# The down projection's seven products in two PSUM banks per visit, with sums kept in PSUM and partial results read between

## The chip, the cores and the metric

The kernel runs on one core of one Trainium2 chip. The metric is the device time of one execution in microseconds, as the median of several runs. The kernel before takes 2273.95 us (three runs, 2269.09 to 2274.33).

The engines named here are TensorE (PE, with its weight loads as PEld), VectorE (DVE), ScalarE (ACT), GpSimd (POOL) and the queue that issues most loads (SP). ScalarE's and GpSimd's own instruction queues issue transfers too.

## The reference

One block of a hybrid network, float32, 512 tokens, model width 2048, feed-forward width 5632. The first part (input projection, a state-space mixer, a three-branch attention, output projection) is not touched. What matters here is the end:

```python
    h = h + mixed @ w_out[l]
    v = rmsnorm(h, ffn_norm_w[l])
    h = h + (jax.nn.silu(v @ w_gate[l]) * (v @ w_up[l])) @ w_down[l]
return rmsnorm(h, final_norm_w)
```

The outputs must match this in float32, so every large product is done as three passes: both factors are split into a high part in the rounded format fp32r and a low part (the remainder), and high x high, high x low and low x high are added.

## The kernel before

**Seven products instead of eight.** In the gate, up and down projections, a 2x2 block product (two blocks of weight rows by two of weight columns, against two halves of 256 tokens) is done by seven products M1 to M7 of sums of blocks, in the manner of Strassen and Winograd. The weight blocks are 11, 12, 21, 22; the sums are S1 = 21 + 22, S3 (from 21 and 11), 11 + S1 (for M6) and 12 + 11 + S1 (for M3, where block 11 already holds the sum). M1 takes 11, M2 12, M5 S1, M7 S3, M4 22. The sums of activations are formed once and kept: for gate/up in the tiles V0, VV (in u) and T, for down in a scratch tensor g_d in device memory.

**Stages.** Up to about 800 us: input projection, mixer, attention and half of the output projection. 800 to 893 us: the other half of the output projection. About 893 to 1792 us: gate/up, 22 tiles u = 0 to 21, each with a gate side (0) and an up side (1), seven products a side, eight k-steps a product. A k-step of gate/up has two matmuls: the high weights against high and low activations together (512 columns) and the low weights against the high ones (256). From about 1792 us: down.

**Down.** 35 visits (table `VISITS`): visit (j, n) adds n k-blocks to output block j. A k-step has three matmuls of 256 columns (lines 1172 to 1174: high x high, high x low, low x high). The first 33 visits run their products in the order `SEQ_D` = M1, M2, M6, M3, M7, M4, M5; the last two visits use `SEQ_END` with a bank for each product, and are interleaved by `put_last`. `BANK_D` says which half (256 columns) of which of a visit's four PSUM banks a product fills. After M1, M6, M7 and M5, when a bank is full, `d_after` and `d_add` have VectorE add it to the accumulators `H[j]` in SBUF: four reads of 512 elements and two of 256 in a visit (the first visit of a block copies with ScalarE). PSUM has eight banks here: six turn round under the names ps_g, ps_s, ps_t (`bank`).

**Order of the work.** From the output projection's second half on, the order of instructions is as written: `run_step` is one product. It first lets `feed` issue loads of g_d, runs `before`, then `prep(i + 2)`: for the product three ahead, `form` does the weight sum if there is one (VectorE, line 134) and the high part (ScalarE, line 122); for the product two ahead, the low part (VectorE, line 125). Then come the product's matmuls, with one `sch.tick()` a k-step, and `after`, its reads of PSUM. `tick` also moves background generators on: `g_forms(u)` forms the seven activation sums of a finished gate/up tile, and its `yield n` waits n k-steps. It ends with a store to g_d from ScalarE's queue (line 1454), six k-steps after the last low part. `silu(u, ...)` is another such generator.

**Gate/up reads.** BANK puts M1, M6, M7, M4 in one bank X, M5 and M3 in R, M2 in W. The results are chained: the next product of the same bank adds on, and ScalarE or VectorE reads the sum so far in between (M1 at line 1379, M6 at 1384, M2 at 1389, M5 at 1395, M7 and M3 by VectorE, M4 at 1411). So the next product in that bank must wait for that read.

**Ring of activations.** The tiles V0, VV and T are reused in down as seven slots for g_d, loaded in two halves (four and three of the seven sums) by `feed`, from ScalarE's queue (line 1548). A slot is loaded once its last reader is done by some steps (table `done`).

**Sums of weights in down.** S1 is formed in place by GpSimd (line 134, POOL) from 21 and 22; S3 by GpSimd in the first six visits, later by an adding transfer from GpSimd's queue (line 1109).

Of the kernel before, what the change touches and what calls it, by code (L numbers as in the profile page):

```python
# [11 lines left out]
ALU = mybir.AluOpType  # L12
# [100 lines left out]
def body(ctx, tc, xT, w_in, w_out, w_gate, w_up, w_down, w1k, w1v, cols, rows, kst, out):  # L113
# [1042 lines left out]
    def run_step(s):  # L1156
# [13 lines left out]
        for k in range(0 if s.wide else n):  # L1170
            ah, al = s.rhs(k)
            pe.matmul(q, h[:, k, :], ah, start=(k == 0), stop=False)  # L1172
            pe.matmul(q, h[:, k, :], al, start=False, stop=False)  # L1173
            pe.matmul(q, l[:, k, :], ah, start=False, stop=(k == s.blk.n - 1))  # L1174
            sch.tick()
# [145 lines left out]
    def banks(which):  # L1321
        got = {}

        def get(p):
            def g():
                b, h = which[p]
                if b not in got:
                    got[b] = bank()
                return got[b], got[b][:, 256 * h:256 * h + 256]
            return g  # L1330
# [32 lines left out]
    def gu_after(u, side, got):  # L1363
        both = u in (0, NP - 1)

        def after(pr):
            def ev(p):
# [7 lines left out]
                c4 = c.rearrange("p (a t) -> p a t", a=4)  # L1375
                if pr == M1:
                    if u:
                        got["W"] = bank()
                    act.activation(got["W"] if u else u2, p, AF.Copy)
                elif pr == M6:  # L1380
                    if u == 0:
                        add(dve, u2, got["W"], u2)
                        add(dve, c4[:, 0], u2[:, lo_h], u2[:, hi_h])
                    act.activation(u2, p, AF.Copy)  # L1384
                elif pr == M2:
                    if u and both:
                        fold(c4[:, 0], p)
                    elif u:
                        act.activation(wv[:, 0, :], p, AF.Copy)
                elif pr == M5:  # L1390
                    if u == 0:
                        dve.tensor_tensor(m5, p, m5, ALU.subtract)
                        add(dve, u2, p, u2)
                    else:
                        act.activation(m5, p, AF.Copy)
                elif pr == M7:
                    add(dve, m5, p, m5)
                    if u == 0:
                        add(dve, c4[:, 1:4:2], wv[:, :, lo_h], wv[:, :, hi_h])
                elif pr == M3:  # L1400
                    if u == 0:
                        act.activation(m5, p, AF.Copy)
                    else:
                        add(dve, u2, p, u2)
                        if both:
                            add(dve, c4[:, 1:4:2], wv[:, :, lo_h], wv[:, :, hi_h])
# [26 lines left out]
    def g_forms(u):  # L1433
# [5 lines left out]
        yield 10  # L1439
        a_hi(sg[:, 0, 0, :], g[:, 0, lo_h])  # L1440
        a_hi(sg[:, 1:3, 0, :], g[:, 1, :].rearrange("p (a t) -> p a t", a=2), scale=-1.0)
# [464 lines left out]
```

## Time and profile before

| | us |
|---|---|
| median of 3 runs | 2273.95 |
| the profiled execution's own time | 2275.06 |
| its span, first to last instruction | 2273.3 |
| PE busy | 2177.7 (96%) |
| PEld busy | 1916.4 (84%) |
| DVE busy | 1822.6 (80%) |
| ACT busy | 1187.4 (52%) |
| POOL busy | 426.1 (19%) |

Mean granted TensorE clock: 0.984. The page gives busy time per engine, the costliest groups, and who released whom; "idle before" of a group is the time that its engine stood still just before, and "waits" list pairs of a waiting instruction and what it waited for, with the total, the number of times and the longest. Matmuls are pipelined, and a matmul's end is modelled: two that follow each other overlap, so the distance of starts says how fast TensorE goes.

### The profile page before, as it was taken

Reading aid. Unit: us, or ns where it says so; the run is one execution under the profiler, and the core shown is the slowest. Engines: PE = TensorE matmul, PEld = TensorE weight load, DVE = VectorE, ACT = ScalarE, POOL = GpSimd, SP = SyncE. Lnnn points to the kernel's source line nnn. Section 1 sums busy time; section 2 is a strip of 40 time slices with the busy share of each in tenths; the row PEclk is TensorE's granted clock in tenths of the full one; section 3 lists DMA queues with packets and bytes.
Section 4 is the critical chain, followed back from the end, with each engine's and each line's share of the span. In section 5 each row is a group of like instructions: output and inputs, shape, how many; then the busy total and the mean of one; then the engine's idle time right before and its main releaser. Section 6 shows DMA issues by size and latency. Waiting matters only on the chain. (4 is left out here: it accounts for less than half of the span.)

```text
span 2273.3 us, 35008 instructions
## 1 busy us (share of the span) xinstructions
PE 2177.7 (96%) x12904; PEld 1916.4 (84%) x12904; DVE 1822.6 (80%) x2858; ACT 1187.4 (52%) x1961; POOL 426.1 (19%) x433
## 2 busy tenths in 40 slices
PE   7999999999989989999999999999999899999996
PEld 5888888888877777888888888888888899999996
DVE  7699766688888667878888788887887798988897
ACT  4564446567666544655555555555555443333453
POOL 2011224223133224000000100001000121221222
PEclk8999999999989999999999999999999999999999
DMA  5222343222413265787878878788787969796974
GB/s 176 93 70 75 128 136 103 75 85 73 137 60 125 69 223 166 227 219 219 236 211 248 219 219 236 211 249 219 219 236 212 333 236 307 189 297 180 300 190 134
DMA packets 168555, 417.17 MB, mean 184 GB/s; under 512 B 16592, under 2 KB 23520, under 8 KB 168384
## 3 DMA queue, kind: packets, MB, share of 16 engines
q1 hardware_dynamic: 99776, 252.24, 33.7%
q0 software_dynamic: 25888, 76.72, 17.2%
q10 hardware_dynamic: 42720, 85.99, 10.5%
q8 instruction: 101, 1.65, 0.3%
q14 instruction: 70, 0.57, 0.1%
HBM read 353.80 MB, written 57.41 MB: 181 GB/s over the span
## 5 line engine op out<-in xcount | busy, mean ns | idle before, releaser
L122 ACT ACTIVATE R<-Z 128x1024 fp32r<-128x1024 f32 (+4 forms) x457 | 420.8, 934 | 442.7 <-DVE Z L134 315.0
L125 DVE TENSOR_TENSOR R<-Z,R 128x1024 fp32r<-128x1024 f32 (+4 forms) x363 | 393.6, 1092 | 41.1 <-ACT R L122 30.5
L232 PE MATMUL ps_g<-u,whi 128*128 128x512 f32 x720 | 286.1, 397 | 0.2 <-DVE h L131 0.2
L234 PE MATMUL ps_g<-u,wlo 128*128 128x512 f32 x720 | 284.4, 395 | 0.0
L233 PE MATMUL ps_g<-u,whi 128*128 128x512 f32 x720 | 283.9, 394 | 0.0
L1168 PE MATMUL ps_s<-u,R 128*128 128x512 f32 (+1 forms) x1152 | 253.4, 349 | 26.8 <-ACT A L1384 26.3
L1168 PEld LDWEIGHTS ps_s<-u,R 128*128 128x128 f32 x1152 | 186.6, 188 | 60.0 <-ACT A L1384 32.9
L125 DVE TENSOR_TENSOR wlo<-wraw,whi 128x512 fp32r<-128x512 f32 x196 | 151.3, 775 | 66.0 <-ACT whi L122 65.4
L122 ACT ACTIVATE whi<-wraw 128x512 fp32r<-128x512 f32 x196 | 122.6, 626 | 134.4 <-PE ps_g L233 89.7
L234 PEld LDWEIGHTS ps_g<-u,wlo 128*128 128x128 f32 x720 | 135.6, 188 | 27.1
L232 PEld LDWEIGHTS ps_g<-u,whi 128*128 128x128 f32 x720 | 135.9, 189 | 26.0 <-DVE h L131 0.5
L233 PEld LDWEIGHTS ps_g<-u,whi 128*128 128x128 f32 x720 | 135.8, 189 | 25.4
L1168 PE MATMUL ps_t<-u,R 128*128 128x512 f32 x592 | 132.5, 350 | 0.0
L134 DVE TENSOR_TENSOR A<-ps_g,A 128x512 f32<-128x512 f32 (+1 forms) x114 | 73.9, 655 | 73.1 <-PE ps_g L1168 39.1
L1168 PE MATMUL ps_g<-u,R 128*128 128x512 f32 (+1 forms) x600 | 131.5, 348 | 0.0
L1168 PE MATMUL ps_g<-T,R 128*128 128x512 f32 (+1 forms) x584 | 126.9, 348 | 0.0
L1168 PE MATMUL ps_s<-T,R 128*128 128x512 f32 (+1 forms) x552 | 123.9, 351 | 0.0
L1172 PE MATMUL ps_g<-u,R 128*128 128x256 f32 (+1 forms) x353 | 115.1, 326 | 9.0 <-ACT R L122 7.1
L122 ACT ACTIVATE R<-A 128x1024 fp32r<-128x1024 f32 (+3 forms) x79 | 74.7, 946 | 92.3 <-DVE A L134 65.2
L1168 PE MATMUL ps_s<-V,R 128*128 128x512 f32 (+1 forms) x568 | 122.7, 347 | 0.0
L125 DVE TENSOR_TENSOR E<-Z,R 128x1024 fp32r<-128x1024 f32 x94 | 114.6, 1219 | 9.4 <-ACT R L122 6.5
L1173 PE MATMUL ps_g<-u,R 128*128 128x256 f32 (+1 forms) x353 | 114.1, 323 | 0.0
(484 smaller groups left out, 5702.8 us busy)
## 6 DMA issues: line engine op xcount, KB each, us to landing
Z<-in_w_gate SPq DMA_DIRECT2D x95, 512.0 KB, 5.5
Z<-in_w_up SPq DMA_DIRECT2D x94, 512.0 KB, 5.1
wraw<-in_w_in SPq DMA_DIRECT2D x164, 256.0 KB, 2.6
g_d<-A ACTq DMA_DIRECT2D x22, 1792.0 KB, 13.9
Z<-in_w_gate POOLq DMA_DIRECT2D x39, 512.0 KB, 5.6
Z<-in_w_up POOLq DMA_DIRECT2D x38, 512.0 KB, 7.4
Z<-in_w_down SPq DMA_DIRECT2D x58, 320.0 KB, 5.4
Z<-in_w_down SPq DMA_DIRECT2D x40, 384.0 KB, 4.1
```

Source lines behind the costliest of these rows:

```text
L122: act.activation(dst, src, AF.Copy, scale=scale)
L125: eng.tensor_tensor(dst, src, f(hi), ALU.subtract)
L134: eng.tensor_tensor(o, a, b, ALU.add)
L232: pe.matmul(p, hi_t[i][:, j, :], ah, start=(k == 0), stop=False)
L233: pe.matmul(p, hi_t[i][:, j, :], al, start=False, stop=False)
L234: pe.matmul(p, lo_t[i][:, j, :], ah, start=False, stop=(k == u.nk - 1))
L1168: pe.matmul(o, w, x, start=start, stop=(k == n - 1 and o is q), skip_group_check=not fresh[0])
L1172: pe.matmul(q, h[:, k, :], ah, start=(k == 0), stop=False)
L1173: pe.matmul(q, h[:, k, :], al, start=False, stop=False)
```

## The change

Down runs its products in the gate/up order `SEQ` = M1, M5, M6, M2, M7, M3, M4, in two banks a visit. In the first bank M6 fills the lower half, M1 the upper half, and M2 adds on to M1. In the second M5 fills the lower half, M3 adds on to it, M7 fills the upper half, M4 adds on to it. VectorE reads M1, M5 and M7 alone (256 elements each) before the next product is added, and M6 with M1+M2, and M5+M3 with M7+M4 (512 each). For that the sums of activations get other signs (`g_forms`) and another order (`G_POS`). Only the first matmul in a bank clears it (`fresh`).

Four things come along. The store to g_d is issued 16 k-steps, not 6, after the last low part. `feed` loads the first halves of the first five ring slots one step after their last reader, where it was three (and for the first two slots counted from a later reader). The first gate/up tile u = 0 runs in the order of `SEQ`, and the pieces of T that it needs (`t_piece`) come at steps 0, 1, 4, 5, 7, 9 instead of 1 to 6. In the last two visits the products get three banks (`BANK_END`), another order (M1, M7, M6, M2, M4, then M5 of both, M3 of both), and the final norm's sums over the first 256 tokens are taken after M5 of the one and turned into a row after M5 of the other.

```diff
-SEQ_D = [M1, M2, M6, M3, M7, M4, M5]
-BANK_D = {M1: (0, 0), M6: (1, 0), M2: (1, 1), M3: (2, 0), M7: (2, 1), M4: (3, 0), M5: (3, 1)}
+BANK_D = {M6: (0, 0), M1: (0, 1), M2: (0, 1), M5: (1, 0), M3: (1, 0), M7: (1, 1), M4: (1, 1)}
-G_POS = [0, 1, 2, 4, 3, 5, 6]
+G_POS = [0, 1, 4, 3, 2, 5, 6]
...
-            pe.matmul(q, h[:, k, :], ah, start=(k == 0), stop=False)
...
+            go = dict(skip_group_check=fresh == [False])
+            pe.matmul(q, h[:, k, :], ah, start=(k == 0 and fresh != [False]), stop=False, **go)
...
     def g_forms(u):
...
-        yield 6
+        yield 16
         nc.scalar.dma_start(g_d[u].rearrange("v p n -> p v n"), f(sg).rearrange("p v s t -> p v (s t)"))
...
-                t_piece(*[(0, 1), (1, 1), (2, 0), (2, 1), (3, 0), (3, 1)][n - 1])
+                t_piece(*PIECES[n])
...
-    both_sides(0, "011 111 0S1 012 112 1S1 0S3 1S3 022 122", [(i, p) for p in (M1, M2, M3) for i in range(2)] +
-               [(i, p) for p in (M6, M5, M7, M4) for i in range(2)])
+    both_sides(0, "011 111 0S1 1S1 012 112 0S3 1S3 022 122", [(i, p) for p in SEQ for i in range(2)])
...
-                at = max(done.get((n - GRING, half), i), later.get(n, 0))
-                if n < 2 and half == 0:
-                    at = done.get((n + 1 - GRING, 0), i)
-                if n < 5 and half == 1:
-                    at = done.get((4 - GRING, 0), i) + n // 2
-                if at + 3 > i:
+                at = max(done.get((n - GRING, half), i), later.get(n, 0)) + 3
+                if n < 5:
+                    at = done.get((n - GRING, 0), i) + 1 if half == 0 else done.get((4 - GRING, 0), i) + 3 + n // 2
+                if at > i:
...
-    def d_add(j, pr, p, first, last):
+    def d_add(j, pr, p, first):
...
         if pr == M1:
             if first:
-                act.activation(H[:, 0, :], p[:, 0:256], AF.Copy)
-                add(dve, H[:, 1, :], p[:, 0:256], H[:, 1, :])
+                act.activation(H[:, 0, :], p[:, hi_h], AF.Copy)
             else:
-                add(dve, H[:, 0:2, :], b2, H[:, 0:2, :])
-        elif pr == M6:
+                add(dve, H[:, 0, :], p[:, hi_h], H[:, 0, :])
+        elif pr == M2:
             add(dve, H[:, 0:2, :], p2, H[:, 0:2, :])
+        elif pr == M5:
+            dve.tensor_tensor(H[:, 4, :], H[:, 4, :], p[:, lo_h], ALU.subtract)
         elif pr == M7:
-            add(dve, H[:, 2:4, :], p2, H[:, 2:4, :])
             add(dve, H[:, 4, :], p[:, hi_h], H[:, 4, :])
-        elif pr == M5:
-            add(dve, H[:, 3:5, :], p2, H[:, 3:5, :])
-            dve.tensor_tensor(H[:, 2, :], H[:, 2, :], p[:, hi_h], ALU.subtract)
+        elif pr == M4:
+            add(dve, H[:, 2:4, :], p2, H[:, 2:4, :])
...
-    SEQ_END = [M1, M2, M6, M7, M4, M5, M3]
+    SEQ_END = [M1, M7, M6, M2, M4, M5, M3]
+    BANK_END = {M6: (0, 0), M1: (0, 1), M2: (0, 1), M5: (1, 0), M3: (1, 0), M7: (2, 0), M4: (2, 0)}
```

Three places show how instructions move. The first is ScalarE's queue in a gate/up tile, around the store to g_d. R<-Z and R<-A are high parts of weights, A<-ps are the reads of PSUM (line 1384 is that of M6, 1389 that of M2). Before:

```order
L122 ACTIVATE A<-A 128x4x256
L1395 ACTIVATE A<-ps_g 128x512
L122 ACTIVATE R<-Z 128x1024
L1454 DMA g_d<-A 128x7x512
L1384 ACTIVATE A<-ps_s 128x512
L122 ACTIVATE R<-Z 128x1024
L1389 ACTIVATE A<-ps_t 128x512
```

The same place now (lines 1383 and 1391 are the reads of M6 and M2):

```order
L121 ACTIVATE A<-A 128x2x2x256
L1393 ACTIVATE A<-ps_g 128x512
L121 ACTIVATE R<-Z 128x1024
L1383 ACTIVATE A<-ps_s 128x512
L121 ACTIVATE R<-Z 128x1024
L1391 ACTIVATE A<-ps_t 128x512
L121 ACTIVATE R<-Z 128x1024
L1449 DMA g_d<-A 128x7x512
```

The store stood ahead of the read of M6; now it stands behind the reads of M6 and M2 and two high parts.

The second place is VectorE in one down visit of five k-blocks, buffers with their numbers. R<-... are low parts, a row without a PSUM tile and without R a sum of weights. Before (banks ps_s_17829, ps_t_17849, ps_g_17888, ps_s_17927):

```order
L134 TENSOR_TENSOR Z_8316<-ps_s_17829,Z_8316 128x512
L125 TENSOR_TENSOR R_8317<-Z_8316,R_8317 128x640 x2
L134 TENSOR_TENSOR Z_8316<-ps_t_17849,Z_8316 128x512
L125 TENSOR_TENSOR R_8317<-E2_15800,R_8317 128x640
L125 TENSOR_TENSOR R_8317<-Z_8316,R_8317 128x640
L134 TENSOR_TENSOR Z_8316<-ps_g_17888,Z_8316 128x512
L134 TENSOR_TENSOR Z_8316<-ps_g_17888,Z_8316 128x256
L125 TENSOR_TENSOR R_8317<-Z_8316,R_8317 128x640
L134 TENSOR_TENSOR Z_8316<-Z_8316 128x640
L125 TENSOR_TENSOR R_8317<-Z_8316,R_8317 128x640
L134 TENSOR_TENSOR Z_8316<-ps_s_17927,Z_8316 128x512
L1602 TENSOR_TENSOR Z_8316<-Z_8316,ps_s_17927 128x256
```

Now (banks ps_g_17910 and ps_s_17929):

```order
L133 TENSOR_TENSOR A_8313<-ps_g_17910,A_8313 128x256
L124 TENSOR_TENSOR R_8317<-Z_8316,R_8317 128x640
L1589 TENSOR_TENSOR A_8313<-A_8313,ps_s_17929 128x256
L133 TENSOR_TENSOR Z_8316<-Z_8316 128x640
L124 TENSOR_TENSOR R_8317<-Z_8316,R_8317 128x640 x2
L133 TENSOR_TENSOR A_8313<-ps_g_17910,A_8313 128x512
L124 TENSOR_TENSOR R_8317<-Z_8316,R_8317 128x640
L133 TENSOR_TENSOR A_8313<-ps_s_17929,A_8313 128x256
L124 TENSOR_TENSOR R_8317<-A_8313,R_8317 128x640
L133 TENSOR_TENSOR A_8313<-A_8313,E2_15801 128x640
L124 TENSOR_TENSOR R_8317<-E2_15801,R_8317 128x640
L133 TENSOR_TENSOR A_8313<-ps_s_17929,A_8313 128x512
```

Three reads of 256 elements and two of 512 stand where four of 512 and two of 256 stood; the read of M7 alone (the first of 256 from ps_s_17929 at line 133) has one low part between it and the read of M6 and M1+M2.

The third place is TensorE in the same visit, the end of M7 and the start of M3, with the engines that a matmul waits for in brackets:

```order
L1172 MATMUL ps_s_17929<-u_94,R_8317 128x256 [waits DMAHW2_49]
L1173 MATMUL ps_s_17929<-u_94,R_8317 128x256
L1174 MATMUL ps_s_17929<-u_94,R_8317 128x256
L1172 MATMUL ps_s_17929<-V0_8321,R_8317 128x256 [waits DVE_49,Activation_49]
L1173 MATMUL ps_s_17929<-V0_8321,R_8317 128x256
```

M3 begins in the bank that M7 has just left, with no product between, and its first matmul now waits for VectorE as well as ScalarE; by the counts of the semaphore, the instruction of VectorE that it waits for is the read of M7 (256 elements of ps_s_17929).

More of the change, by code (lines that the diff above doesn't have):

```diff
@@ L1171, in run_step @@
             ah, al = s.rhs(k)
[L1172 to L1174 removed]
+            go = dict(skip_group_check=fresh == [False])
+            pe.matmul(q, h[:, k, :], ah, start=(k == 0 and fresh != [False]), stop=False, **go)
+            pe.matmul(q, h[:, k, :], al, start=False, stop=False, **go)
+            pe.matmul(q, l[:, k, :], ah, start=False, stop=(k == n - 1), **go)
             sch.tick()
@@ L1326, in g @@
                 b, h = which[p]
-                if b not in got:
+                new = b not in got
+                if new:
                     got[b] = bank()
-                return got[b], got[b][:, 256 * h:256 * h + 256]
+                return got[b], got[b][:, 256 * h:256 * h + 256], new
             return g
@@ L1497, in both_sides @@
             b, sums = q["form"][p]
-            if u == 0 and p in (M3, M6):
-                sums = [(q["11"], q["S1"]), (q["12"], q["11"])] if p == M3 else ()
             if u and n == 0:
@@ L1502, in both_sides @@
             else:
-                before = start_ff(n) if u == 0 and n < 7 else None
+                before = start_ff(n) if u == 0 and (n == 0 or n in PIECES) else None
             s = Step(b, v_rhs(p), bk[side][1](p), after=ev, before=before, sums=sums,
@@ L1612, in ev @@
             def ev(p):
-                d_add(j, pr, p, first, last)
-                if last and pr == M6:
+                d_add(j, pr, p, first)
+                if last and pr == M2:
                     add_x(j)
-                if last and pr == M5:
+                if last and pr == M4:
                     squares(j)
@@ L1683, in ev @@
                     half_sq(j, 0)
+                elif pr == M5:
+                    dve.tensor_tensor(H[:, 4, :], H[:, 4, :], q, ALU.subtract)
+                    (half_row if second else half_sum)(lo_h)
                 elif pr == M3:
@@ L1712, in body @@
     last = []
-    def one_bank():
-        t = bank()
-        return t, t[:, 0:256]
     def put_last(ns, which):
-        for j, a, q, af in which:
-            for n in ns:
+        for n in ns:
+            for j, a, q, af, bk in which:
                 blk, sums = q["form"][SEQ_END[n]]
-                Step(blk, g_rhs(SEQ_END[n], a), one_bank, after=af(SEQ_END[n]), sums=sums)
+                Step(blk, g_rhs(SEQ_END[n], a), bk(SEQ_END[n]), after=af(SEQ_END[n]), sums=sums)
     for v, (j, a, b) in enumerate(visits):
@@ L1735, in body @@
                 P2["order"] = [i for i in range(NJ) if all(i != x[0] for x in last)] + [x[0] for x in last]
-                for x in last:
-                    put_last(range(5, 7), [x])
+                put_last(range(5, 7), last)
             continue
-        for n, p in enumerate(SEQ_D):
+        for n, p in enumerate(SEQ):
             blk, sums = q["form"][p]
```

70 lines of the change are left out of this document (28 added, 42 removed).

## The prediction

> **What bounds the kernel now.** I read the page first, then busy time by stage, then TensorE's waits in each stage, then the order of time around one wait of each kind.
>
> ```profile
> span 2273.3 us, 35008 instructions
> PE 2177.7 (96%) x12904; PEld 1916.4 (84%) x12904; DVE 1822.6 (80%) x2858; ACT 1187.4 (52%) x1961; POOL 426.1 (19%) x433
> ...
> core 0: us, PE busy (x) PEld busy (x) DVE busy (x) ACT busy (x) POOL busy (x), PEclk, DMA share, GB/s
> 945.00:1770.00 825.00, 798.70 (x4546) 694.30 (x4546) 671.35 (x693) 453.93 (x589) 69.98 (x81) 1.00 0.80 226
> 1770.00:1820.00 50.00, 43.48 (x266) 39.99 (x265) 39.33 (x52) 19.03 (x33) 9.48 (x6) 0.90 0.97 359
> 1820.00:2240.00 420.00, 414.02 (x3445) 408.76 (x3444) 365.47 (x504) 172.74 (x258) 96.49 (x75) 1.00 0.80 237
> ```
>
> TensorE is the bound, and the number of its matmuls does not change. So only three things can move the time: the gaps in which it stands, its clock, and the tail. Gate/up (945 to 1770) has 26.3 us of gaps, down (1820 to 2240) 6.0 us, and the entry to down between them 6.5 us at a clock of 0.90. Down therefore has little to give: even a perfect order there saves single microseconds, while VectorE (365 of 420 us) is close behind TensorE.
>
> Who ends the gaps of gate/up is one line, and what that line waits for is another:
>
> ```profile
> PEld ps_s L1168 <- ACT A L1384: 32.9, 21, 2.7
> ...
> ACT A L1384 <- DVE A L125: 31.1, 20, 1.6
> ```
>
> The first row says that a weight load of gate/up stood 21 times for ScalarE's read of M6. The second says that this read stood 20 times for a low part that VectorE writes into A, which is none of its own operands. The order of time around one of them explains it:
>
> ```profile
> 1274.89 1.07 ACT L122 ACTIVATE R<-Z 128x1024 fp32r<-128x1024 f32 x1 [0.59 <-DVE Z L134]
> 1275.57 1.31 PE L1168 MATMUL ps_t<-u,R 128*128 128x256 f32 x7
> 1275.85 1.22 DVE L125 TENSOR_TENSOR A<-A 128x1024 fp32r<-128x1024 f32 x1
> ...
> 1276.99 1.22 DVE L125 TENSOR_TENSOR R<-Z,R 128x1024 fp32r<-128x1024 f32 x1
> 1277.10 0.37 ACTq L1454 DMA_DIRECT2D g_d<-A  x1
> 1277.51 0.60 ACT L1384 ACTIVATE A<-ps_s 128x512 f32<-128x512 f32 x1 [1.55 <-DVE A L125]
> ...
> 1278.16 0.19 PEld L1168 LDWEIGHTS ps_s<-u,R 128*128 128x128 f32 x1 [1.59 <-ACT A L1384]
> 1278.16 0.50 PE L1168 MATMUL ps_s<-u,R 128*128 128x512 f32 x1 [1.28 <-ACT A L1384]
> ```
>
> The store to g_d waits in ScalarE's queue until the last low part of the activation sums ends (1275.85 + 1.22 = 1277.07). The read of M6 stands behind it, though M6 is long finished, and M7, which adds to the same bank, cannot start: TensorE ran out of M2 at 1276.9 and starts again at 1278.16. This comes once in a gate/up tile.
>
> **The change part by part.** The sum is made against the profiled execution's own 2275.06 us.
>
> *Gate/up, the store 16 k-steps after the low part.* It now stands behind the reads of M6 and M2. The read of M6 can start when the high part ahead of it ends (1274.89 + 1.07 = 1275.96) and takes 0.60, so it ends near 1276.6, before TensorE has finished M2. The store itself finds its low part done. Next late would be M7's low part or the read of M2. A k-step is 825/(4546/2) = 0.36 us at most, so M7 takes 2.9 us, and VectorE ended the low part that comes after the store's within 1.2 us of 1277.07; nothing there is due before M7 ends. Cover for the store: g_d is read only in down. What the stops cost is between the matmuls' 26.3 us of gaps and the weight loads' 32.9 us; a stop also costs the overlap of load and matmul, so I take 31 us. Bounds: -33, and -20 if part of it comes back at another read. **-31.**
>
> *Down, VectorE's reads.* What TensorE waits for in down today are low parts:
>
> ```profile
> PEld ps_t L1174 <- DVE R L125: 4.2, 10, 0.6
> PEld ps_g L1174 <- DVE R L125: 4.1, 7, 1.1
> PEld ps_s L1174 <- DVE R L125: 1.8, 5, 0.6
> ...
> L134 DVE TENSOR_TENSOR A<-ps_g,A 128x512 f32<-128x512 f32 x38 | 26.0, 684 | 6.2 <-PE ps_g L1174 5.9
> L1602 DVE TENSOR_TENSOR A<-A,ps_g 128x256 f32<-128x256 f32 x11 | 4.5, 409 | 0.0
> L125 DVE TENSOR_TENSOR R<-E,R 128x512 fp32r<-128x512 f32 x7 | 4.8, 681 | 0.0
> ```
>
> Reads cost 4 x 0.684 + 2 x 0.409 = 3.55 us a visit before and 2 x 0.684 + 3 x 0.409 = 2.60 now, 0.95 less, 31 us of VectorE over 33 visits. Only the 10.1 us of waits can come from it. I take **-8**, bounds -10 and 0.
>
> *Down, M3 right behind M7 in one bank.* This is a new wait, once in each of 33 visits: VectorE reads the upper half of the bank, M3 writes the lower half, and M3's first matmul waits for that read. (The other two new waits, M6 for the read of M1 and M7 for that of M5, have a whole product and two products between, 1.8 and 3.5 us at five k-blocks, against a read of 0.41: nothing.) All of TensorE's queue stands behind M3. The trace has each link:
>
> ```profile
> 2061.37 0.28 PE L1173 MATMUL ps_g<-T,R 128*128 128x256 f32 x1
> 2061.49 0.28 PE L1174 MATMUL ps_g<-T,R 128*128 128x256 f32 x1
> 2061.61 0.28 PE L1172 MATMUL ps_s<-u,R 128*128 128x256 f32 x1
> ...
> 2061.81 0.69 DVE L134 TENSOR_TENSOR A<-ps_g,A 128x512 f32<-128x512 f32 x1 [0.42 <-PE ps_g L1174]
> ...
> 2117.32 1.81 POOL L134 TENSOR_TENSOR Z<-Z 128x512 f32<-128x512 f32 x1 [9.93 <-DMA Z<-in_w_down]
> 2117.89 1.79 DVE L125 TENSOR_TENSOR R<-Z,R 128x512 fp32r<-128x512 f32 x1
> 2119.74 0.38 PE L1174 MATMUL ps_g<-u,R 128*128 128x256 f32 x1 [0.44 <-DVE R L125]
> ...
> 2119.96 0.28 PE L1172 MATMUL ps_g<-V,R 128*128 128x256 f32 x1
> ```
>
> From the start of a bank's last matmul to the read: 2061.81 - 2061.49 = 0.32. The read: 0.41. From VectorE's end to the matmul: 2119.74 - (2117.89 + 1.79) = 0.06. Against that stands the usual distance of starts, 0.12. The first matmul after a stop is followed by the next after 0.22, 0.10 more. Together 0.32 + 0.41 + 0.06 - 0.12 + 0.10 = 0.77 us, x 33 = 25.4 us. That is the bound from below: VectorE idle when M7 ends. M7 lasts 15 x 0.12 = 1.8 us in a visit of five k-blocks; VectorE has in it the read of 512 (0.68) and a low part (about 0.8), so it is mostly in time. Not when GpSimd is adding: beside the addition at 2117.32 a low part of 512 took 1.79 against 0.68. If that fell on every visit, 33 x (0.77 + 1.11) = 62 us, the bound from above. It is once a visit and lasts about 2 of 13 us, so I stay near the lower end: **+29.**
>
> *The first gate/up tile and the entry to down.*
>
> ```profile
> PEld ps_t L1168 <- DVE E L125: 3.6, 1, 3.6
> ...
> 910.00:914.00 4.00, 4.00 (x18) 3.44 (x16) 3.76 (x4) 3.05 (x4) 0.66 (x1) 0.57 0.46 142
> 1798.00:1802.00 4.00, 4.00 (x23) 4.00 (x22) 2.39 (x4) 2.01 (x5) 0.00 (x0) 0.58 1.05 384
> 1809.00:1815.00 6.00, 5.68 (x26) 5.68 (x27) 5.04 (x7) 1.05 (x2) 2.59 (x2) 0.50 0.98 361
> ...
> PEld ps_s L1172 <- DMA u<-g_d: 3.1, 1, 3.1
> PEld ps_g L1172 <- DMA u<-g_d: 2.0, 1, 2.0
> PEld ps_g L1174 <- DVE R L125: 2.0, 1, 2.0
> ```
>
> In u = 0 TensorE stands 3.6 us for a low part behind the T pieces, and then runs four microseconds at a clock of 0.57 (1.7 lost): 5.3 in reach. The pieces are now spread over nine steps, and two sums of weights that stood ahead come later. **-4**, bounds -5 and +4 (the same wait at another product, since T's first piece is now due at step 2).
>
> At the entry three waits make 7.1 us, and the slow clock behind them 4 x 0.42 + 6 x 0.50 = 4.7. The first halves of the ring slots are now asked for 4, 4, 2, 2 and 2 steps of 2.9 us earlier; a stage whose DMA share is 0.97 gets them spread out. On ScalarE these issues stand behind reads of the same products, so they hold little back. The second halves are asked for as before, and the third wait is one for a second half. **-5**, bounds -12 and +5, for S1 is now needed for the second product, where it was first needed for the third.
>
> *Tail.* Both M3 now stand last, so the first outputs have one product less (18 matmuls, 2.1 us) to hide behind: **+1**, bounds -1 and +2.
>
> Sum: -31 - 8 + 29 - 4 - 5 + 1 = -18, so 2275.06 - 18 = 2257. The median shown lies 1.1 under the profiled execution: **2256 us**.
>
> A rule speaks against this part. The Trainium skill ("PSUM — Partial Sum Buffer", the section on bank collisions) says that two engines must be kept apart by bank and group of partitions, not by address; so M3's wait could not be lifted though the columns differ. No run here shows what happens without it.
>
> **The rivals.** *VectorE late for M7 in every visit.* The GpSimd rows speak for it; against it, M7 covers what stands ahead. Price: the upper bound, +33 on the forecast, 2289 us. It is slower than before from 0.77 + 25/33 = 1.5 us a visit on.
>
> *The stop in gate/up moves.* ScalarE still waits for the store, or M7 for its low part, at another product: up to +31, 2287 us. Against it: the low part ends 0.2 us after M2, and the store is ten k-steps later.
>
> *S1 comes late.* M5 needs it one product earlier than M6's sum did:
>
> ```profile
> POOL Z L134 <- DMA Z<-in_w_down: 104.4, 13, 15.7
> ...
> DVE Z L134 <- POOL Z L134: 2.9, 2, 1.7
> ```
>
> GpSimd's sums wait for loads, and VectorE waited for them only twice; if a product (1.8 us) were missing in half the visits, 16 x 1.8 = 29: 2285 us.
>
> *The clock falls after the new stops.* A stretch at half clock costs about 1.7 us (910 to 914 above), x 33 = 56: 2312 us. Against it: gate/up had twenty stops of 1.3 us at a clock of 1.00. The Trainium skill ("TensorE: Matmul & The Clock Gate", the section on PSUM-queue depth-cycling) tells of a kernel whose short stops between groups of matmuls made the clock swing; by that rule this rival would win, and the trace disagrees so far.
>
> *M3 does not stand at all*, should read and write of two halves overlap: 2256 - 29 = 2227 us. The program names the wait.
>
> **How the numbers follow.** Forecast 0.66, its own range 2245 to 2267; VectorE late 0.09; stop moved 0.06; S1 late 0.07; clock 0.03; no wait 0.03; the rest, unforeseen, 0.06. With 2240 to 2274 about two in ten is left out, mostly above. This kernel's measurement tells 0.3% (6.8 us) from no change. Faster: 0.62 of the forecast, 0.03, and 0.05 of the rest and of milder rivals, 0.70; slower: most of the four dear rivals, 0.15; the same 0.15.
>
> **What would show it.** Right: no row "ACT A <- DVE A" in front of gate/up's reads, and 945 to 1770 shortened by some 31 us with TensorE near 100% busy; in down a row of 33 waits of TensorE for VectorE's read of 256 elements, 0.6 to 0.9 us each, the waits for low parts nearly gone, VectorE under 80% busy. Wrong: these waits at 1.5 us, a granted clock under 1.00 in down, waits for GpSimd or for ScalarE's high parts at M5, or gate/up still with a stop per tile.

## The result, and the profile after

The changed kernel takes 2294.81 us (median of five runs, 2285.64 to 2298.89) against 2273.95 (five runs, 2269.09 to 2276.11). The ratio is 1.0087, with a 95% interval of 1.0061 to 1.0113: it is slower by about 21 us. Forecast were 2256 us, with a range of 2240 to 2274. A second time, beside other kernels, it took 2288.03 against 2273.41 (1.0069, 1.0052 to 1.0085). The head of the profile page:

```profile
span 2293.0 us, 35062 instructions
PE 2180.6 (95%) x12904; PEld 1917.8 (84%) x12904; DVE 1792.4 (78%) x2811; ACT 1183.3 (52%) x1961; POOL 425.2 (19%) x433
```

TensorE is still the bound, with as many matmuls, and VectorE does 30 us less. The time lies in TensorE's gaps and in its clock. Busy time by stage (sum of a stretch, engines, granted clock, DMA share):

```profile
945.00:1770.00 825.00, 814.16 (x4642) 709.22 (x4643) 680.67 (x704) 454.66 (x598) 73.04 (x83) 1.00 0.82 237
1770.00:1820.00 50.00, 42.91 (x335) 41.37 (x334) 41.89 (x57) 21.15 (x37) 13.03 (x8) 0.97 0.80 283
1820.00:2120.00 300.00, 281.66 (x2331) 277.23 (x2332) 225.37 (x310) 108.73 (x160) 56.20 (x44) 1.00 0.76 235
2120.00:2240.00 120.00, 104.42 (x815) 102.42 (x813) 85.98 (x116) 49.63 (x75) 27.84 (x24) 0.94 0.68 182
```

Gate/up improved: TensorE stands 10.8 of 825 us, where it stood 26.3. Down got worse: it stands 18.3 us in the first 300 and 15.6 us in the next 120, there with a clock of 0.94, where in 420 us it had stood 6.0 at a clock of 1.00.

These windows hold different work in the two kernels. So I also cut both traces by work: a gate/up tile has 224 matmuls, a down visit of n k-blocks 21 n, and the distance from the first matmul of one stage to that of the next is its time.

| stage, us | before | after | difference | forecast |
|---|---|---|---|---|
| up to gate/up | 893.0 | 892.5 | -0.5 | 0 |
| tile 0 | 46.2 | 40.7 | -5.5 | -4 |
| tiles 1 to 20 | 813.6 | 795.9 | -17.7 | -31 |
| tile 21 | 39.2 | 40.7 | +1.5 | in the next |
| down, visits 0 to 32 | 431.5 | 466.2 | +34.7 | -8 + 29 - 5 = +16 |
| down, the last two visits | 34.7 | 40.3 | +5.6 | +1 with the next |
| from the last matmul of down to the end | 15.1 | 16.8 | +1.7 | |
| span | 2273.3 | 2293.0 | +19.7 | -18 |

**Down: the stop at M3.** TensorE's waits in the first 33 visits, by tile and releaser (total, times, longest; L133 writing A or Z is VectorE's read of PSUM):

```profile
PE ps_g L1172 <- DVE A L133: 12.3, 11, 2.6
PE ps_s L1172 <- DVE A L133: 9.2, 9, 2.6
PE ps_t L1172 <- DVE A L133: 6.8, 8, 1.5
PE ps_t L1172 <- DVE Z L133: 3.3, 2, 2.7
PE ps_s L1172 <- DVE Z L133: 1.2, 2, 0.6
```

These are 32 waits from 1795 us on; that of the first visit lies before. By distances of starts, less the usual 0.1145 us, M3's first matmul comes 39.8 us late over the 33 visits: 0.77 to 0.86 us in 22 of them, 17.2 together, and 22.6 us in the other 11. In time order, an ordinary one in a visit of five k-blocks:

```profile
1925.94 0.28 PE L1174 MATMUL ps_g<-T,R 128*128 128x256 f32 x1
1926.26 0.42 DVE L133 TENSOR_TENSOR A<-ps_g,A 128x256 f32<-128x256 f32 x1
1926.83 0.36 PE L1172 MATMUL ps_g<-u,R 128*128 128x256 f32 x1 [0.61 <-DVE A L133]
1927.03 0.28 PE L1173 MATMUL ps_g<-u,R 128*128 128x256 f32 x1
```

From M7's last matmul to M3's first are 0.89 us; that less 0.12 is 0.77. VectorE's read ends at 1926.68, and M3 starts 0.15 us after that, in this visit and in all 33. And a long one, in visit 30, which finishes an output block (POOL and VectorE first, then TensorE):

```profile
2187.24 0.69 DVE L133 TENSOR_TENSOR Z<-ps_s,Z 128x512 f32<-128x512 f32 x1 [0.51 <-PE ps_s L1174]
2187.97 0.42 DVE L133 TENSOR_TENSOR Z<-Z 128x256 f32<-128x256 f32 x1
2188.15 1.93 POOL L133 TENSOR_TENSOR Z<-Z,E 128x768 f32<-128x768 f32 x1 [0.46 <-DMA E<-in_w_down]
2188.31 2.31 DVE L1599 TENSOR_TENSOR Z<-Z 128x512 f32<-128x512 f32 x1
2190.55 0.95 DVE L124 TENSOR_TENSOR R<-Z,R 128x768 fp32r<-128x768 f32 x1
2191.41 0.41 DVE L133 TENSOR_TENSOR Z<-ps_t,Z 128x256 f32<-128x256 f32 x1
...
2189.04 0.28 PE L1174 MATMUL ps_t<-V,R 128*128 128x256 f32 x1
...
2191.97 0.35 PE L1172 MATMUL ps_t<-T,R 128*128 128x256 f32 x1 [2.66 <-DVE Z L133]
```

M7 ended with the matmul at 2189.04, and its read (2191.41) could start only after two additions of the block's end (256 elements at 2187.97, 512 at line 1599) and a low part. Line 1599 lasts 2.31 us beside GpSimd's addition; five others of the same line in down have a mean of 0.684.

**Gate/up: another stop.** The row "ACT A <- DVE A" is gone, but of TensorE's waits from 945 to 1770 us one row for the read of M6 stays:

```profile
PE ps_s L1167 <- ACT A L1383: 9.7, 13, 2.1
```

By starts, the old stop (M7 on the gate side) fell from 29.5 us in 20 tiles to 0.8 in one; a new one, at M7 on the up side, takes 11.0 us in 12 tiles, and -29.5 + 0.8 + 11.0 is the -17.7 of the table. What stands ahead of that read, in one tile:

```profile
1078.66 1.06 ACT L121 ACTIVATE R<-A 128x1024 fp32r<-128x1024 f32 x1 [2.03 <-DMA A<-in_w_up]
1079.62 0.62 ACT L1420 ACTIVATE A<-A 128x512 f32<-128x512 f32 x1
1080.14 0.62 ACT L1421 ACTIVATE A<-A 128x512 f32<-128x512 f32 x1
...
1080.79 1.23 DVE L130 TENSOR_TENSOR A<-A,rrow 128x1024 f32<-128x1024 f32 x1 [2.02 <-ACT A L1421]
1081.93 1.22 DVE L133 TENSOR_TENSOR Z<-Z 128x1024 f32<-128x1024 f32 x1
...
1083.25 1.07 ACT L121 ACTIVATE R<-Z 128x1024 fp32r<-128x1024 f32 x1 [2.01 <-DVE Z L133]
1084.23 0.57 ACT L1383 ACTIVATE A<-ps_s 128x512 f32<-128x512 f32 x1
...
1084.85 0.51 PE L1167 MATMUL ps_s<-u,R 128*128 128x512 f32 x1 [0.46 <-ACT A L1383]
```

ScalarE stands 2 us for a load of up weights; SiLU (lines 1420 and 1421) waits behind its high part, VectorE's product with the row scale (line 130) for SiLU, the weight sum of M3 behind that product, the high part for the sum, the read of M6 behind the high part, and M7 for the read.

(The sum is that of M3, formed three products ahead; the expectation of experiment six calls it M6's.) The late load is that of S3 for M7, an adding transfer from GpSimd's queue. It lands no later than before: 25.0 us on the mean after the first matmul of its tile, before the change 24.8. What has moved is the up side, which begins 19.6 us after that matmul, before 21.1. ScalarE gets there sooner and waits: for loads of up weights 42 us between 945 and 1770, before 7 us.

**The last two visits.** M7 stands second there now:

```profile
2248.69 0.28 PE L1174 MATMUL ps_g<-V,R 128*128 128x256 f32 x1
2252.42 1.58 ACT L121 ACTIVATE R<-Z 128x768 fp32r<-128x768 f32 x2 [10.56 <-DMA Z<-in_w_down]
2253.32 0.58 PE L1172 MATMUL ps_s<-T,R 128*128 128x256 f32 x1 [4.35 <-ACT R L121]
```

M1 of the last visit ends, and M7 waits 4.4 us for the high part of S3, whose load has only just landed.

### The profile page after: what moved, and what is told of

It is laid out like the page before. It is cut to its first block, busy times and chain, and to the rows that moved or that the text cites. A ratio compares the mean times of both kernels' runs of the same rounds, so it can differ in the third digit from the quotient of the medians.

```text
span 2293.0 us, 35062 instructions
## 1 busy us (share of the span) xinstructions
PE 2180.6 (95%) x12904; PEld 1917.8 (84%) x12904; DVE 1792.4 (78%) x2811; ACT 1183.3 (52%) x1961; POOL 425.2 (19%) x433
## 4 chain that ended last, share of the span: by engine, by line
PE 83%; DVE 7%; DMA 5%; issue 3%; ACT 2%; POOL 0%; ACTq 0%; SPq 0%; DVEq 0%; POOLq 0%
PE ps_s L1167 18%; PE ps_g L1167 10%; PE ps_g L231 7%; PE ps_g L232 7%; PE ps_g L233 7%; PE ps_t L1167 4%; PE ps_g L1172 3%; PE ps_g L1174 3%; PE ps_g L1173 3%; PE ps_s L1172 2%; PE ps_t L1172 2%; PE ps_s L1174 2%; PE ps_s L1173 2%; PE ps_v L879 2%; PE ps_t L1174 2%
## 5 line engine op out<-in xcount | busy, mean ns | idle before, releaser
L124 DVE TENSOR_TENSOR R<-Z,R 128x1024 fp32r<-128x1024 f32 (+4 forms) x368 | 389.1, 1061 | 43.2 <-ACT R L121 26.3
L232 PEld LDWEIGHTS ps_g<-u,whi 128*128 128x128 f32 x720 | 135.8, 189 | 25.4
L1167 PE MATMUL ps_t<-u,R 128*128 128x512 f32 (+1 forms) x600 | 131.5, 348 | 0.0
L1167 PE MATMUL ps_g<-u,R 128*128 128x512 f32 x584 | 131.4, 350 | 0.0
L133 DVE TENSOR_TENSOR A<-ps_g,A 128x512 f32<-128x512 f32 (+1 forms) x102 | 64.7, 635 | 84.8 <-PE ps_g L1174 42.2
L1172 PE MATMUL ps_g<-u,R 128*128 128x256 f32 (+1 forms) x355 | 117.6, 331 | 13.3 <-ACT R L121 7.4
L1173 PE MATMUL ps_g<-u,R 128*128 128x256 f32 (+1 forms) x355 | 116.2, 327 | 0.0
## 6 DMA issues: line engine op xcount, KB each, us to landing
g_d<-A ACTq DMA_DIRECT2D x22, 1792.0 KB, 15.1
```

The costliest lines, as they stand in the source:

```text
L124: eng.tensor_tensor(dst, src, f(hi), ALU.subtract)
L133: eng.tensor_tensor(o, a, b, ALU.add)
L232: pe.matmul(p, hi_t[i][:, j, :], al, start=False, stop=False)
L1167: pe.matmul(o, w, x, start=start, stop=(k == n - 1 and o is q), skip_group_check=not fresh[0])
L1172: pe.matmul(q, h[:, k, :], ah, start=(k == 0 and fresh != [False]), stop=False, **go)
L1173: pe.matmul(q, h[:, k, :], al, start=False, stop=False, **go)
```

## The experiments

Each was compared with the kernel before on the same chip. The times of stages are cut from the traces as in the table above; where an expectation gives 34.1 or 39.7 us for the last two visits, it counts five matmuls less than the table's 34.7 and 40.3.

**One: only the store, on the kernel before.**

```diff
-        yield 6
+        yield 16
         nc.scalar.dma_start(g_d[u].rearrange("v p n -> p v n"), ...)
```

> The kernel before with one edit: the store to g_d is issued 16 k-steps after the last low part, not 6. Theory A (the store's stop is gone, and a second, hidden one comes up in its place: a weight load that comes late holds ScalarE and VectorE on the up side, as the changed kernel shows with 12 stops, 11.0 us in all): the twenty tiles u = 1 to 20 take 813.6 us before and about 796 us now, the rest is as before, 2256 us in all, with stops of M7 on the up side. Rival B (those 12 stops come from another part of the change, the new order of activation sums or of the first tile): no stop is left, the twenty tiles take about 784 us, 2244 us in all.

2253.92 us against 2274.66 (0.9908, 0.9894 to 0.9923). Tiles 1 to 20 take 791.7 us, and the wait for the read of M6 is there too:

```profile
PE ps_s L1168 <- ACT A L1384: 6.0, 8, 1.5
```

By starts these are 9 stops of M7 on the up side, 7.1 us. So theory A holds: the store's stop is worth 29 us, and part of it is given back at a stop that no other part of the change makes. The one edit alone is 21 us faster than before; what the rest of the change does costs about twice as much as that.

**Two: M7 one product earlier, and M3 last, in the same two banks.**

```diff
-        for n, p in enumerate(SEQ):
+        for n, p in enumerate([M1, M5, M6, M7, M2, M4, M3]):
...
-            if n == 3:
+            if n == 4:
                 done.update(((i, 0), s.i) for i in range(a, b))
...
-        elif pr == M4:
+        elif pr == M3:
             add(dve, H[:, 2:4, :], p2, H[:, 2:4, :])
...
-                if last and pr == M4:
+                if last and pr == M3:
                     squares(j)
```

> The changed kernel with down's products in the order M1, M5, M6, M7, M2, M4, M3, the two banks and the five reads as they are: between M7 and the next product of its bank stands M2 now. Theory A (M3's wait for the read of M7, 39.8 us over 33 visits, is what made down slower, and the slow clock after the long ones comes with it): down's 33 visits take 466 us in the changed kernel and about 421 to 426 us now, 2250 us in all, no row of TensorE waiting for VectorE's read of 256. Rival B (VectorE's work in a visit is the limit, and the wait only shows it): TensorE waits for low parts or at M5 and M1 instead, and the time stays above 2275 us.

2270.21 us against 2274.66 (0.9975, 0.9964 to 0.9985). No stop at M3 is left, and the 33 visits take 440.7 us, not 466.2. But it is 20 us short of theory A: M7 now waits 11.8 us in eight visits, for the high part of S3 or for a late read of M5, M4 3.8 us in two, and the last two visits take 45.7. So the wait was the cause, but a product cannot be pulled ahead for nothing when its weights have no slack.

**Three: the order as it is, M7 and M4 in a bank of their own.**

```diff
-BANK_D = {M6: (0, 0), M1: (0, 1), M2: (0, 1), M5: (1, 0), M3: (1, 0), M7: (1, 1), M4: (1, 1)}
+BANK_D = {M6: (0, 0), M1: (0, 1), M2: (0, 1), M5: (1, 0), M3: (1, 0), M7: (2, 0), M4: (2, 0)}
...
         elif pr == M7:
-            add(dve, H[:, 4, :], p[:, hi_h], H[:, 4, :])
+            add(dve, H[:, 4, :], p[:, lo_h], H[:, 4, :])
+        elif pr == M3:
+            add(dve, H[:, 2, :], p[:, lo_h], H[:, 2, :])
         elif pr == M4:
-            add(dve, H[:, 2:4, :], p2, H[:, 2:4, :])
+            add(dve, H[:, 3, :], p[:, lo_h], H[:, 3, :])
```

> The changed kernel with its order of products, but M7 and M4 in a third bank of the visit, so M3 adds to M5's bank alone; reads are M1, M5, M7, M3 and M4 at 256 elements and one of 512, 0.14 us more of VectorE a visit. Theory A (the wait is for the shared bank): as with M7 moved, about 2250 us, no stop at M3. Rival B (the wait comes from the order, M3's operands or VectorE's load): stops at M3 remain, above 2280 us.

2256.53 us against 2274.66 (0.9922, 0.9905 to 0.9938), near theory A's 2250. TensorE's largest waits in the 33 visits, behind the first:

```profile
PE ps_g L1172 <- ACT R L121: 3.7, 2, 3.2
PE ps_g L1174 <- DVE R L124: 2.8, 3, 1.5
PE ps_g L1172 <- DVE A L133: 2.1, 4, 1.2
PE ps_g L1172 <- DVE Z L133: 1.4, 1, 1.4
```

No visit stops at M3, with one read more, and the 33 visits take 429.7 us, less than before the change (431.5). The wait was for the shared bank. What is left at line 133 is M4 waiting for the read of M7, by starts 4.8 us in six visits, five of which end a block. The last two visits take 43.5 us, which is no more than in some other profiles with this end (40.3 to 45.7); M7's wait is 7.2 us, in the others 4.5 to 4.8, and why is open.

**Four: a block's closing sums after the read of M7, not before.**

```diff
                 d_add(j, pr, p, first)
-                if last and pr == M2:
+                if last and pr == M7:
                     add_x(j)
```

> The changed kernel with one move: in the last visit of an output block, the two additions that spread the first accumulator to the others (256 and 512 elements, VectorE) come after the read of M7, not before it. Theory A (they are what makes the read of M7 late in visits 27 to 32, where the stop at M3 is 1.2 to 2.8 us against 0.77 elsewhere): these six stops fall to about 0.8, 9 us less, and the slow stretches of the clock behind them go, 3 to 5 us more; about 2282 us. Rival B (GpSimd's addition, which stretches VectorE's operations beside it, makes them late): the long stops stay, less than 3 us are saved, 2292 us or more.

2280.75 us against 2274.66 (1.0025, 1.0013 to 1.0037). The stops at M3 fall from 39.8 to 29.5 us; in visits 27 to 32 from 1.2, 2.4, 2.1, 2.8, 2.8 and 2.8 us to 0.8, 1.3, 1.1, 0.8, 0.8 and 0.8. No slow stretch of the clock is left between 1779 and 2217. Theory A holds. The stops that stay long (1.3 to 1.7 us in visits 0, 9, 21, 26 and 28) do not stand behind these sums: in 9, 21 and 26 a low part of VectorE lasts 1.5 to 2.5 us beside an addition of GpSimd, and visit 28 has three k-blocks, so that M7 lasts only 1.0 us.

**Five: the last two visits as before.**

```diff
-    SEQ_END = [M1, M7, M6, M2, M4, M5, M3]
-    BANK_END = {M6: (0, 0), M1: (0, 1), M2: (0, 1), M5: (1, 0), M3: (1, 0), M7: (2, 0), M4: (2, 0)}
+    SEQ_END = [M1, M2, M6, M7, M4, M5, M3]
+    BANK_END = {p: (p, 0) for p in SEQ_END}
...
-                put_last(range(5, 7), last)
+                for x in last:
+                    put_last(range(5, 7), [x])
```

(with each product read alone, and the row of the first 256 tokens at the read of M3 of the one)

> The changed kernel, with the last two visits in the order and banks of the kernel before (M1, M2, M6, M7, M4, and M5, M3 of the one before M5, M3 of the other). In the changed kernel these two visits take 39.7 us and the rest to the end 16.8 us, before 34.1 and 15.1. Theory A (M7 stands second now and needs the sum S3, whose load lands 4.5 us too late; a slow stretch of the clock follows): 34 and 15 us again, 2287 us in all. Rival B (the load is late whatever the order, and the wait moves to the fourth product): less than 2 us gained, 2293 us.

2281.00 us against 2275.27 (1.0022, 1.0013 to 1.0032). The last two visits take 34.3 us and the rest 15.0, 7.8 less than in the changed kernel's profile, and no wait for S3 is left: theory A. (Of the other 7 us by which its profile is shorter 5 lie in gate/up, where it has 9 stops on the up side and not 12.)

**Six: in gate/up, the product with the row scale eight k-steps later.**

```diff
-        yield 6
+        yield 14
         mul(dve, c2, c2, rr)
         sch.flags.add(("r", u))
```

> The changed kernel, with VectorE's product of SiLU with the row scale in gate/up put off by 8 k-steps, so that the weight sum of M6 goes ahead of it on VectorE. Theory A (the 12 stops at M7 of the up side, 11.0 us, come by a chain: a late weight load holds ScalarE's SiLU, VectorE's product waits for SiLU, the weight sum waits behind the product, ScalarE's high part for the sum, and the read of M6 behind that high part): the stops go but for 1 or 2, gate/up is 8 to 10 us shorter, 2286 us in all. Rival B (the late load alone holds ScalarE long enough): the stops stay, less than 3 us, 2293 us.

2283.95 us against 2275.27 (1.0035, 1.0023 to 1.0047). In gate/up one wait for the read of M6 is left:

```profile
PE ps_s L1167 <- ACT A L1383: 0.7, 1, 0.7
```

Tiles 1 to 20 take 784.3 us, 11.6 less. The same place in time order, with the load even later (2.68 us of wait) than in the tile shown above:

```profile
1079.16 1.23 DVE L133 TENSOR_TENSOR Z<-Z 128x1024 f32<-128x1024 f32 x1
1079.65 1.07 ACT L121 ACTIVATE R<-A 128x1024 fp32r<-128x1024 f32 x1 [2.68 <-DMA A<-in_w_up]
...
1081.90 1.22 DVE L130 TENSOR_TENSOR A<-A,rrow 128x1024 f32<-128x1024 f32 x1
1082.14 1.06 ACT L121 ACTIVATE R<-Z 128x1024 fp32r<-128x1024 f32 x1
1083.09 0.59 ACT L1383 ACTIVATE A<-ps_s 128x512 f32<-128x512 f32 x1
```

The sum no longer waits for SiLU, and the late load is absorbed: the chain was the cause, the load only its start.

**Seven: the ring's loads as late as before.**

```diff
-                at = max(done.get((n - GRING, half), i), later.get(n, 0)) + 3
-                if n < 5:
-                    at = done.get((n - GRING, 0), i) + 1 if half == 0 else done.get((4 - GRING, 0), i) + 3 + n // 2
-                if at > i:
+                at = max(done.get((n - GRING, half), i), later.get(n, 0))
+                if n < 2 and half == 0:
+                    at = done.get((n + 1 - GRING, 0), i)
+                if n < 5 and half == 1:
+                    at = done.get((4 - GRING, 0), i) + n // 2
+                if at + 3 > i:
```

> The changed kernel with the loads of the ring slots as late as in the kernel before. Theory A (the prediction's: the earlier first halves shorten the entry to down by some 5 us): tile 21 and the first visit are 3 to 5 us longer, 2299 us. Rival B (the waits at the entry are for other things, and the earlier loads only crowd those of weights in tile 21, which is 1.5 us longer than before): no change or 1 to 2 us less, 2294 us.

2288.39 us against 2275.27 (1.0055, 1.0039 to 1.0070), which cannot be told from the changed kernel's 1.0069. Tile 21 and the first four visits take 97.4 us with the late loads and 97.7 with the early ones. Tile 21 is 1.5 us shorter, as rival B had it, and M1 of the first visit then waits 4.3 us for the ring. The early loads are worth nothing on the whole: what they take from that wait comes back in tile 21 and at other waits.

**Eight: the edits of three, four, five and six together.**

> The changed kernel with four edits together: M7 and M4 in a third bank, the sums at a block's end after M7, the last two visits as in the kernel before, and the product in gate/up put off. Theory A (each wait is a loss by itself): 2256.5 us of the three-bank kernel, less 5 for the stops at M4 behind the sums, less 8 for the last two visits, less 8 in gate/up: about 2236 us. Rival B (with these gone the loads of weights become the limit): waits for loads at M7 and M5 take half back, 2247 us or more.

2238.58 us against 2275.27 (0.9835, 0.9820 to 0.9850), theory A within 3 us and faster than both kernels. The head of its page:

```profile
span 2237.3 us, 34969 instructions
PE 2168.9 (97%) x12904; PEld 1914.2 (86%) x12904; DVE 1793.2 (80%) x2848; ACT 1182.6 (53%) x1961; POOL 425.0 (19%) x433
```

Tiles 1 to 20 take 784.4 us, the 33 visits 426.4, the last two 35.2, the rest 15.2.

**Nine: the two edits in gate/up on the kernel before, down untouched** (the diffs of one and six).

> The kernel before with two edits in gate/up alone: the store 16 k-steps after the low part, and the product of SiLU with the row scale put off by 8 k-steps. Down, its entry, the first tile and the last visits are as before. Theory A (the waits of gate/up are independent of down): tiles 1 to 20 at 784 us, 2247 us in all, and the distance to the four edits together (2238.6) is what the new order of down in three banks, its entry and the first tile are worth, some 8 us. Rival B (without the stops in gate/up the old down meets late loads): 2252 us or more, no gain on the store alone.

2242.42 us against 2273.41 (0.9867, 0.9849 to 0.9885), better than theory A's 2247. So 31 of the 37 us of the kernel with four edits come from two numbers in gate/up, and all else that is new (tile 0, the entry, down, its end) is worth about 4 to 6: the 33 visits take 430.2 us in the old order and 426.4 in the new.

**Ten: the loads of the first five ring slots from GpSimd's queue.** The edits of eight, and:

```diff
-                nc.scalar.dma_start(f(G[n][:, r]).rearrange("p v s t -> p v (s t)"),
+                (nc.gpsimd if n < 5 else nc.scalar).dma_start(f(G[n][:, r]).rearrange("p v s t -> p v (s t)"),
```

> The four edits together, and the loads of the first five ring slots issued from GpSimd's queue in place of ScalarE's. Theory A (at the entry ScalarE's high part of M6 stands behind such a load that waits for its slot, and TensorE waits 3.8 us at M6 and loses 2.3 us to the slow clock after it): both go or shrink to a third, 2234 us. Rival B (the data of the ring is what comes late, from whichever queue, or GpSimd's sums now stand behind the loads): 2238 us or more.

2237.60 us against 2273.41 (0.9839, 0.9823 to 0.9854): as eight, within what can be told. In the changed kernel and in eight, M6 of the first visit waits (the first row, of the changed kernel); here that wait is gone, and another of the same size stands in its place (the second row, of this kernel):

```profile
PE ps_s L1172 <- ACT A L1583: 2.8, 1, 2.8
```

```profile
PE ps_s L1174 <- DVE R L124: 3.2, 1, 3.2
```

Tile 21 and the first four visits take 93.8 us, against 93.3 in eight. That is nearer to rival B: with one wait gone, another stands in its place.

**Eleven: the changed kernel again**, beside nine and ten.

> The changed kernel itself, beside the two others on one chip: 2285 to 2299 us, with the 33 stops at M3 of 37 to 40 us together. What moves between its executions is the count of late loads in gate/up (4 to 11 us in the profiles of the kernels that share its gate/up) and the slow stretches after stops of 2 us and more.

2288.03 us; the stops at M3 make 40.0 us. Tiles 1 to 20 take 793.1 us with 10 stops on the up side (8.3 us). The profile compared above, with 12 stops and 11.0 us, is one of the longer executions.

**Twelve: the end with both M3 last, M7 in fourth place.** The edits of eight, and:

```diff
-                for x in last:
-                    put_last(range(5, 7), [x])
+                put_last(range(5, 7), last)
```

(and the row of the first 256 tokens after M5 of the second again)

> The four edits together, but with the end of the changed kernel: M5 of both last visits, then M3 of both, the sums over the first 256 tokens after M5 of the one and their row after M5 of the other; M7 stays fourth. It parts the two things that the change does in the last two visits. Theory A (what costs there is only M7 standing second, the order of the last four is worth about nothing, as the prediction's +1): last two visits 34 to 35 us and 15 to 17 us to the end, 2237 to 2241 us. Rival B (the end costs of itself, first outputs hidden behind one product less): 53 us or more for both, 2242 us or more.

2239.30 us against 2274.50 (0.9846, 0.9829 to 0.9862). The last two visits take 34.5 us and the rest 15.8, 50.3 together against 50.4 in eight. So the order of the last four products is worth nothing either way. What is left as the cost in the last two visits is M7 in second place, where it stood for S3; the three banks there, which experiment five took back too, were not tried alone.

## Why the prediction was wrong, point by point

The forecast was 18 us less than before, and the profiled execution is 19.7 longer. Four steps of the sum failed: that after the store nothing else is late at a read of M6 (13.3 us), that VectorE is mostly in time for M7 (10.8), that the end has only one product less to hide behind (6.3), and that no stop moves the clock (5.9).

**Gate/up, -31: the step that failed is "Next late would be M7's low part or the read of M2".** The mechanism was right, the sum too large by 8 to 13. The store's stop went as told (29.5 us in 20 tiles, now 0.8), but 4 to 11 us come back on the up side in the profiles of the kernels that share this gate/up. The sum named its lower bound for just this case ("-20 if part of it comes back at another read") and then came close to the upper end. What was missed: the next late is the read of M6 on the up side. The old stop also gave ScalarE and VectorE 1.5 us in a tile in which a late load could be made up. I looked only at what stands behind the store, not at what other chain ends at a read of M6. Experiment six showed that chain, and that one number takes it away. The rival "the stop in gate/up moves" had the place, another product, but not the chain.

**Low parts, -8: right.** Between 1820 and 2240 us the weight loads' waits for low parts fell from 10.1 to 2.3 us.

**M3 behind M7, +29: the step that failed is "it is mostly in time".** In 22 of 33 visits the stop is 0.77 to 0.86 us. That this is the forecast's floor is luck. Two of its links came as reckoned, 0.33 us to the read and 0.42 for it; but the matmul follows the read after 0.15 us, not 0.06, and the 0.10 that the floor held for the matmul after that comes on top, 0.08 each time. These are 2.7 us in all, which no sum of stops here contains.

The other 11 were priced by GpSimd's addition alone. What VectorE has ahead of M7's read was counted in an ordinary visit; in one that ends a block it has two additions more (0.42 and 0.68). Put behind that read, they give back 8.6 us over six visits (experiment four), with what GpSimd had stretched there: in visits 30 to 32 one operation of VectorE lasted 2.3 to 2.6 us. That the 33 stops then make 29.5 us and the forecast said 29 is in part the same luck. The first visit's stop (1.79 us) stands behind VectorE's work for the last gate/up tile.

The rival "VectorE late for M7" was thus true in a third of the visits. The prediction says that this rival makes the kernel slower from 1.5 us a visit on; since its forecast already held 29/33 = 0.88, that should be 0.88 + 25/33 = 1.64. Measured are 39.8/33 = 1.21: these stops alone would not have made it slower.

**GpSimd's part was real, and its price right.** In visit 20:

```profile
2045.53 1.83 POOL L133 TENSOR_TENSOR Z<-Z,E 128x768 f32<-128x768 f32 x1 [10.83 <-DMA E<-in_w_down]
2045.74 2.44 DVE L124 TENSOR_TENSOR R<-A,R 128x768 fp32r<-128x768 f32 x1
2048.11 0.41 DVE L133 TENSOR_TENSOR A<-ps_g,A 128x256 f32<-128x256 f32 x1
```

A low part of this size takes 0.95 us elsewhere; here the read of M7 stands behind 2.44, and M3 stops 1.62. Visits 9, 21 and 26 are of the same kind. Over 0.77 the four cost 3.6 us, as much as the forecast's 29 has over its floor of 25.4. The 512-element addition of 2.31 us beside GpSimd's 1.93, against 0.684 alone, is the same stretch in visit 30. The Trainium skill ("SBUF — State Buffer", the section "Who interferes with whom") says that a VectorE instruction with two inputs in SBUF and a GpSimd instruction that reads SBUF exclude each other, the one that comes first holding the port for its whole length. The trace agrees: GpSimd starts at 2188.15 and ends at 2190.08, and VectorE's addition, begun at 2188.31, ends 0.54 us after that.

**The clock, chance 0.03: half right.** The many stops of 0.77 us did not move it (1.00 from 1820 to 2120). Stops of 2 us and more did, though not each:

```profile
2192.00:2195.00 3.00, 3.00 (x26) 3.00 (x27) 2.33 (x3) 0.85 (x1) 0.00 (x0) 1.00 0.86 159
...
2211.00:2214.00 3.00, 3.00 (x17) 3.00 (x17) 1.41 (x2) 0.84 (x1) 0.00 (x0) 0.53 0.97 213
...
2230.00:2233.00 3.00, 3.00 (x16) 3.00 (x16) 0.70 (x1) 0.00 (x0) 0.00 (x0) 0.50 0.93 224
```

These follow stops of 2.8 us at 2189.0, 2206.8 and 2226.0: not after the first, but after the second and third TensorE ran at half clock. (The granted clock is the third number from the end.) In down the stretches behind the stops at 2129.6, 2206.8 and 2226.0 cost 1.7, 1.6 and 2.7 us (the distances of matmuls above the usual one), 5.9 us that no term held.

**The entry, -5: the size nearly right by luck, the reason wrong.** Tile 21 and the first four visits took 96.8 us before and 97.7 after; without the stops at M3 in them (4.3 us) it is 93.4, and 93.2 was measured in three banks. But experiment seven shows that the earlier loads have no part in it. The sum also held that M6's wait for the read of M1 costs nothing, for a product stands between; in the first visit ScalarE makes that read, behind other work, and M6 stood 2.8 us. **Tile 0, -4**, gave -5.5 here and -3.0 to -5.5 in all profiles with this tile 0.

**The tail, +1: wrong by 6.** The outputs behind one product less cost nothing measurable (experiment twelve). What was not seen is the other move in the same lines: M7 goes from fourth to second place, and S3 is the last sum that is ready. Its wait of 4.5 us and the slow stretch behind it (2.0 us) are most of the 7.8 us that experiment five took back. The rival "S1 late" asked this question of the wrong sum: in the 33 visits M5 nowhere stood for S1.

**Together.** No single rival decided it. The prediction missed the profiled execution's time by 37.7 us (2294.81 against 2257.06). Of these 13.3 lie in gate/up, 10.8 at M3, 6.3 in the tail, 5.9 in the clock in down and 1.6 at the entry; less 2 for tile 0 and the stages before it they make 36. All the large ones point the same way: at each something was taken as hidden and its cover was thinner than counted.

**What stays open.** In down, ScalarE waits longer for loads of weights in the new order (before, then after):

```profile
ACT R L122 <- DMA Z<-in_w_down: 11.0, 6, 2.7
```

```profile
ACT R L121 <- DMA Z<-in_w_down: 36.0, 6, 10.6
```

(10.6 of the 36.0 are the wait for S3 in the last two visits.) With four edits they are 23.4 us, and at visit 10 M7 still stands 3.5 us for S3. Blocks 11 and 12 are held until M3, which is sixth now and was fourth, so their places come free later; that this is the cause is argued, not shown. Why S3 of the up side lands 24.1 us into one tile and 26.7 us into another was not tried either.

## What to carry to other kernels

When products are chained in one PSUM bank and the sum so far is read between, put another product between the one that is read and the next in that bank, or give them two banks; one adjacent pair cost 0.85 us each time at best, with the slower second matmul, and whatever the reading engine had ahead of it at worst. Price such a wait in each kind of visit, the ones that close a block too, with everything that stands ahead of the read on its queue. When a stop is removed, follow every chain that ends at the same instruction, since the engines behind it lose their rest; and when a product is moved, ask for the last of its operands, not the first.

## What the runs showed of the hardware

How long a stop of TensorE the clock bears: over the fourteen profiles I took every distance of matmul starts in gate/up behind its first tile and in down that was over 0.6 us above the usual one, and called it followed by a slow stretch when at least eight matmuls within the next 6 us came at 1.4 to 2.3 times their usual distance. Of some 340 stops of 0.6 to 1.9 us about 15 were followed, of some 47 of 1.9 to 3.2 us about 30, of 19 longer ones all; the counts move by a few with what is taken as usual. A stretch lasted 1 to 5.5 us and cost 0.6 to 2.7 us, most often 1.5 to 1.7. The Trainium skill ("TensorE: Matmul & The Clock Gate", the section "What's actually happening") has the clock fall after at least one idle window of about 3.4 us, in windows that run on by themselves; the runs show it after stops of 2 us as well, though not every time. Its section on PSUM-queue depth-cycling tells of a kernel in which short stops made the clock swing, without their length; the 22 short stops here, of 0.77 to 0.86 us, did not.
